# The FFN of a decoder block in two phases, each by Strassen's seven half products

## The chip, the cores and the metric

The kernel runs on one core of a Trainium2 chip. The metric is the device time of one execution in microseconds (us). Of the core's engines, TensorE (PE) multiplies matrices, VectorE (DVE), ScalarE (ACT) and GpSimd (POOL) work element by element, and SyncE (SP) issues the transfers (DMA). SBUF is the on-chip memory, PSUM holds TensorE's sums, DRAM is outside.

## The reference, cut to what matters

T = 1024 tokens, D = 1024. A layer norm and a mixer come first; the change leaves them as they are, up to the layer norm LN1. Then:

```
x = layer_norm(ALPHA * x + (1 + gt_a) * y, ln1_g, ln1_b)
h = x * (1 + sc_f) + sh_f
u = causal_dwconv(h @ w_up, conv_w) + conv_b      # [1024, 5632], three taps along the tokens
gate, val = split(u, 2, axis=-1)
y = (silu(gate) * val) @ w_down                   # [1024, 2816] @ [2816, 1024]
out = layer_norm(ALPHA * x + (1 + gt_f) * y, ln2_g, ln2_b)
```

## The kernel before

Every large product is done in three matmuls: each operand is split into a rounded part (hi) and a remainder (lo), and lo·hi, hi·lo and hi·hi are added in PSUM. Making a split costs a cast on ACT (L157) and a difference on POOL (L158).

LN1 ends in `ln1(t)` for the eight token tiles t; its last step is the ACT instruction L1198. `h2_of(t)` then transposes LN1's output on TensorE (L1207), scales it (L1214 on DVE, L1211 on ACT) into a tile of its own (`qm` or `km`), and splits it into `aH` and `aL`. The last two token tiles are transposed in the middle of the first matmuls of the FFN.

The FFN has 44 column blocks of w_up with 128 columns each: 22 gate blocks and 22 value blocks. `up_products` does one block: two token halves x 8 k-tiles x 3 matmuls of 128x512 (L1231 to L1233). `up` adds the convolution out of PSUM (ACT L1281, DVE L1284 twice), `pair(f)` does the silu (L1289), multiplies (L1291) and splits. `wdown` scales a block of w_down by the adaLN gate (L1300) and splits it. After every two f (four in the last group) the down products are done for all eight token tiles (L1334 to L1336) and added into `acc` (L1340; L1346 in the last group). `acc` already holds the residual, which POOL has made there (L1316, L1320). In the last group each tile's LN2 follows (L1346 to L1363). There are 2112 matmuls of 128x512 for the up products and 1056 (in their size) for the down products.

TensorE's order is that of the program; the other engines' instructions are placed by the framework's scheduler, and each engine runs its list in order. SP has one queue in order.

Of the kernel before, what the change touches and what calls it, by code (L numbers as in the profile page):

```python
# [88 lines left out]
def build(ctx, tc, out, cst, x, c, ln0_g, ln0_b, w_ada, b_ada, w_in, dn_conv, dn_a_log, dn_dt_bias,  # L89
# [1134 lines left out]
    ups = {}

    def up_products(blk, split=cols_of):
        hi, lo = split(w_up, blk * P)
        pp = ups[blk] = pup.tile([P, T], F32, tag="up", name=nm("up"), bufs=2)
        for sl in HS:
            for k in range(NK):  # L1230
                PE.matmul(pp[:, sl], lo[:, k, :], aH[:, k, sl], start=(k == 0), stop=False)  # L1231
                PE.matmul(pp[:, sl], hi[:, k, :], aL[:, k, sl], start=False, stop=False)  # L1232
# [152 lines left out]
```

## Time and profile before

| what | value |
|---|---|
| time, median of 3 runs | 1478.91 us (1477.97 to 1479.74) |
| span of the profiled execution | 1480.0 us |
| TensorE busy | 1414.6 us (96%) |
| DVE, ACT, POOL busy | 800.9, 452.0, 554.5 us |
| first matmul of the FFN, last matmul | 728.81, 1470.00 us |

The profiled execution is 1.1 us longer than the median. Busy time is what an engine spent in instructions, including what an instruction waited for inside itself. A share of the whole span averages over the mixer (up to 728 us), where several engines are busy, and the FFN.

### The profile page before, as it was taken

How to read it: one execution, taken by the hardware profiler on the slowest of the kernel's cores; microseconds unless marked ns; L12 is line 12 of the kernel's file. 1: busy time of each engine (PE TensorE's matmuls, PEld its weight loads, DVE VectorE, ACT ScalarE, POOL GpSimd, SP SyncE). 2: the span in 40 equal slices, each digit the busy share in tenths (PEclk: the TensorE clock that was granted, in tenths of full speed). 3: DMA queues.
4: the chain of work that ended last, by engine and by line, in shares of the span. 5: the costliest groups of instructions: out<-in, count | busy, mean ns of one | idle time of the engine just before them, and what ended most of it. 6: DMA issues, size and time to landing. Idle time of an engine off the chain costs nothing.

```text
span 1480.0 us, 17961 instructions
## 1 busy us (share of the span) xinstructions
PE 1414.6 (96%) x7037; PEld 1130.3 (76%) x7037; DVE 800.9 (54%) x1557; ACT 452.0 (31%) x658; POOL 554.5 (37%) x334
## 2 busy tenths in 40 slices
PE   6796999999998999999999999999999999999997
PEld 4565777788786787778778888888888888888886
DVE  7876954677447235867944343434434343434348
ACT  4356221233334432532541212121221212121322
POOL 2674211121115775431347374133231324133235
PEclk9888999999988998999999999999999999999999
DMA  9556312131204553353021212011111102011103
GB/s 320 148 155 187 70 39 57 32 81 33 69 11 157 179 176 114 122 165 99 15 69 39 64 43 71 29 58 57 44 50 36 58 29 71 29 58 56 30 15 114
DMA packets 144090, 120.20 MB, mean 81 GB/s; under 512 B 24067, under 2 KB 119167, under 8 KB 144005
## 3 DMA queue, kind: packets, MB, share of 16 engines
q1 hardware_dynamic: 144005, 119.05, 26.6%
q8 instruction: 55, 0.90, 0.3%
q14 instruction: 30, 0.25, 0.1%
HBM read 104.05 MB, written 14.98 MB: 80 GB/s over the span
## 4 chain that ended last, share of the span: by engine, by line
PE 78%; DVE 15%; issue 2%; ACT 1%; POOL 1%; DMA 1%; SPq 0%; POOLq 0%; DVEq 0%; ACTq 0%
PE up L1233 11%; PE up L1231 11%; PE up L1232 11%; PE pp L622 6%; PE pp L624 5%; PE pp L623 5%; PE down L1336 5%; PE down L1335 5%; PE down L1334 5%; DVE rq L139 1%; DVE mac L236 1%; DVE rq L140 1%; PE dn L864 1%; DVE ob L651 1%; PE pp L1182 1%
## 5 line engine op out<-in xcount | busy, mean ns | idle before, releaser
L158 POOL TENSOR_TENSOR wlo<-wst,whi 128x1024 fp32r<-128x1024 f32 x71 | 171.2, 2413 | 380.3 <-ACT whi L157 379.8
L1231 PE MATMUL up<-aH,wlo 128*128 128x512 f32 x688 | 272.2, 396 | 0.0
L1232 PE MATMUL up<-aL,whi 128*128 128x512 f32 x688 | 271.8, 395 | 0.0
L1233 PE MATMUL up<-aH,whi 128*128 128x512 f32 x688 | 271.8, 395 | 0.0
L622 PE MATMUL pp<-aH,wlo 128*128 128x512 f32 x432 | 191.2, 442 | 8.4 <-DVE ob L651 6.5
L1340 DVE TENSOR_TENSOR ob<-down,ob 128x512 f32<-128x512 f32 x144 | 97.0, 689 | 171.0 <-PE down L1336 168.9
L1284 DVE SCALAR_TENSOR_TENSOR cv<-up,colC,cv 128x1023 f32<-128x1023 f32 x88 | 112.8, 1281 | 126.0 <-ACT cv L1281 124.4
L624 PE MATMUL pp<-aH,whi 128*128 128x512 f32 x432 | 177.1, 410 | 0.0
L623 PE MATMUL pp<-aL,whi 128*128 128x512 f32 x432 | 176.4, 408 | 0.0
L1232 PEld LDWEIGHTS up<-aL,whi 128*128 128x128 f32 x688 | 129.8, 189 | 30.3
L1233 PEld LDWEIGHTS up<-aH,whi 128*128 128x128 f32 x688 | 129.8, 189 | 30.3
L1231 PEld LDWEIGHTS up<-aH,wlo 128*128 128x128 f32 x688 | 129.9, 189 | 30.2
L1281 ACT ACTIVATE cv<-up,colC 128x1024 f32<-128x1024 f32 x44 | 53.1, 1207 | 265.6 <-PE up L1233 265.6
L1336 PE MATMUL down<-wdhi,ghi 128*128 128x512 f32 (+1 forms) x322 | 125.9, 391 | 0.0
L1335 PE MATMUL down<-wdhi,glo 128*128 128x512 f32 (+1 forms) x322 | 125.7, 390 | 0.0
L1334 PE MATMUL down<-wdlo,ghi 128*128 128x512 f32 (+1 forms) x322 | 121.1, 390 | 0.0
L158 POOL TENSOR_TENSOR wdlo<-wdst,wdhi 128x1024 fp32r<-128x1024 f32 x20 | 56.8, 2841 | 143.9 <-ACT wdhi L157 143.9
L622 PEld LDWEIGHTS pp<-aH,wlo 128*128 128x128 f32 x432 | 85.3, 197 | 30.0 <-DVE ob L651 5.4
L624 PEld LDWEIGHTS pp<-aH,whi 128*128 128x128 f32 x432 | 85.2, 197 | 20.5
L623 PEld LDWEIGHTS pp<-aL,whi 128*128 128x128 f32 x432 | 85.7, 198 | 14.2 <-issue 0.5
L157 ACT CAST whi<-wst 128x1024 fp32r<-128x1024 f32 x71 | 73.9, 1041 | 53.7 <-issue 23.9
L1300 DVE TENSOR_TENSOR wdst<-wdst,gate 128x1024 f32<-128x1024 f32 x22 | 27.5, 1248 | 114.5 <-DMA wdst<-in_ffn_w_down 114.5
(451 smaller groups left out, 2338.2 us busy)
## 6 DMA issues: line engine op xcount, KB each, us to landing
wst<-in_ffn_w_up SPq DMA_DIRECT2D x44, 512.0 KB, 3.8
wst<-in_w_in SPq DMA_DIRECT2D x28, 512.0 KB, 3.9
K<-in_w_ada SPq DMA_DIRECT2D x48, 256.0 KB, 3.4
wdst<-in_ffn_w_down SPq DMA_DIRECT2D x22, 512.0 KB, 3.5
wada<-in_w_ada SPq DMA_DIRECT2D x8, 1024.0 KB, 7.0
xt<-in_x SPq DMA_DIRECT2D x8, 512.0 KB, 9.1
ob<-in_w_ada SPq DMA_DIRECT2D x16, 256.0 KB, 4.3
qd<-in_x SPq DMA_DIRECT2D x16, 256.0 KB, 3.0
```

Of the source, the lines that this page charges most:

```text
L158: eng.tensor_tensor(lo, st, hi.bitcast(F32), op=ALU.subtract)
L622: PE.matmul(pp, lo[:, k, :], aH[:, k, sl], start=(k == 0), stop=False)
L623: PE.matmul(pp, hi[:, k, :], aL[:, k, sl], start=False, stop=False)
L624: PE.matmul(pp, hi[:, k, :], aH[:, k, sl], start=False, stop=(k == NK - 1))
L1231: PE.matmul(pp[:, sl], lo[:, k, :], aH[:, k, sl], start=(k == 0), stop=False)
L1232: PE.matmul(pp[:, sl], hi[:, k, :], aL[:, k, sl], start=False, stop=False)
L1233: PE.matmul(pp[:, sl], hi[:, k, :], aH[:, k, sl], start=False, stop=(k == NK - 1))
L1284: V.scalar_tensor_tensor(t[:, sh:], pp[:, :T - sh], w(j), t[:, sh:], op0=ALU.mult, op1=ALU.add)
L1334: PE.matmul(pds[sl], gh[:, ct(t)], wl[:, sl], start=(i == 0), stop=False)
L1335: PE.matmul(pds[sl], gw[:, ct(t)], wh[:, sl], start=False, stop=False)
L1336: PE.matmul(pds[sl], gh[:, ct(t)], wh[:, sl], start=False, stop=(i == len(grp) - 1))
L1340: V.tensor_tensor(o[:, sl], pds[sl], o[:, sl], op=ALU.add)
```

## The change

It replaces the FFN. Strassen's scheme makes the product of two 2x2 block matrices from seven half-size products in place of eight, and takes sums of blocks on both sides for it.

Phase 1 goes through the 22 f. The 2x2 blocks are: of h, two token halves and two k halves; of w_up, the k halves and the pair of gate block f and value block f. `product(f, i)` is one of the seven products, 4 k-tiles x 3 matmuls, in the order 1, 6, 2, 5, 7, 3, 4; products 2, 3 and 4 go on in the PSUM bank of 1, 5 and 7 after `carry` has read that. `weights(f + 1)` makes the sums of weight blocks and their splits one f ahead (four differences on DVE, five splits and that of the gate block). The operand sums of h are made once, ahead of f = 0, in `acc` itself, where h2 now lies transposed; LN1's output goes to DRAM first (`ax2`). `carry` collects on DVE and ACT into rows of `acc` (seven rows taken in turn, four for each f), does the convolution, silu and product, and for every odd f `sums` stores the seven left operands of the second phase to DRAM (`dS`), four of them after sums on POOL.

Phase 2 has 77 steps: seven products i, in the order 1, 5, 6, 7, 4, 3, 2, by eleven j, each with 4 token tiles x 3 matmuls. `entry(i, j)` loads the left operand from `dS`, loads and combines w_down blocks, and splits both; it runs five steps ahead of the matmuls. `residual` loads LN1's output again and adds the scaled sum to it. The last product goes token tile by token tile, with LN2 behind each.

```diff
-        h2 = mt([P, NK, P], "km" if t % 2 else "qm")
+        nc.sync.dma_start(rowt(ax2, t), xh)
...
+                    V.tensor_scalar(xh[:, ct(k)], pt[:, j, :], AB2[:, 0, k:k + 1], AB2[:, 1, k:k + 1],
+                                    op0=ALU.mult, op1=ALU.add)
+            if t >= NT // 2 and q == 0:
+                continue
+            qs = slice(q * 4, q * 4 + 4)
+            h2 = xh[:, HS[q]].rearrange("p (k c) -> p k c", c=P)
+            S.copy(aH[:, qs, ct(t)], h2)
+            eng = V if t >= NT - 2 else G
+            eng.tensor_tensor(aL[:, qs, ct(t)], h2, aH[:, qs, ct(t)].bitcast(F32), op=ALU.subtract)
...
+    def product(f, i, n):
+        if i in (2, 3, 4) and (f >= 3 or i != 2):
+            pb, first_ = prod[f, {2: 1, 3: 5, 4: 7}[i]], False
+        else:
+            pb, first_ = bank(n), True
+        prod[f, i] = pb
+        hi, lo = opB[f, i]
+        for k in range(4):
+            ah, al = opA[i](k)
+            o = pb if len(ah.shape) == 2 else pb.rearrange("p (t c) -> p t c", c=P)
+            for w, a, flags in ((lo, ah, (first_ and k == 0, False)), (hi, al, (False, False)), (hi, ah, (False, k == 3))):
+                PE.matmul(o, w[:, k, :], a, start=flags[0], stop=flags[1], skip_group_check=not first_)
...
+    def split_s(i, s, eng):
+        if i not in s_hi:
+            s_hi[i] = ft([P, 4, 512], "sh", 2, F32R)
+        s_lo = ft([P, 4, 512], "sl", 4, F32R)
+        S.copy(s_hi[i], s)
+        eng.tensor_tensor(s_lo, s, s_hi[i].bitcast(F32), op=ALU.subtract)
+        opA[i] = (lambda k, hi=s_hi[i], lo=s_lo: (hi[:, :, ct(k)], lo[:, :, ct(k)]))
+    V.tensor_tensor(A22, A21, A22, op=ALU.add)
+    split_s(5, A22, G)
+    V.tensor_tensor(A21, A11, A21, op=ALU.subtract)
+    V.tensor_tensor(A11, A22, A11, op=ALU.subtract)
+    split_s(6, A11, V)
+    split_s(7, A21, G)
+    V.tensor_tensor(A12, A12, A11, op=ALU.subtract)
...
+    def weights(f):
+        B12, B22 = ft([P, 4, P], "vq", 3), ft([P, 4, P], "vq", 3)
+        nc.sync.dma_start(B22, wcols(NF + f, 1))
+        nc.sync.dma_start(B12, wcols(NF + f, 0))
+        st = raw.pop(f) if f in raw else gate_block(f)
+        yield
+        T3 = t3_tile()
+        V.tensor_tensor(T3, B22, B12, op=ALU.subtract)
+        V.tensor_tensor(B12, B12, st[:, KH[0], :], op=ALU.subtract)
+        split_q(f, 3, B22)
+        yield
+        V.tensor_tensor(B22, B22, B12, op=ALU.subtract)
+        split_q(f, 6, B22)
+        yield
+        split_q(f, 5, B12)
+        V.tensor_tensor(B22, st[:, KH[1], :], B22, op=ALU.subtract)
+        yield
+        split_q(f, 7, T3)
+        yield
+        split_q(f, 4, B22)
+    dS = {i: dram.tile([NF // 2, P, 512], F32, name=f"dS{i}") for i in range(1, 8)}
...
+    def conv(blk, cb):
+        t = row()
+        w = lambda j: colC[:, j * 44 + blk:j * 44 + blk + 1]
+        S.activation(t, cb, AF.Identity, bias=w(3), scale=w(2))
+        for j in (1, 0):
+            sh = 2 - j
+            V.scalar_tensor_tensor(t[:, sh:], cb[:, :T - sh], w(j), t[:, sh:], op0=ALU.mult, op1=ALU.add)
+        return t
...
+    def sums(j):
+        e, o = gs.pop(2 * j), gs.pop(2 * j + 1)
+        a11, a21, a12, a22 = e[:, HS[0]], e[:, HS[1]], o[:, HS[0]], o[:, HS[1]]
+        for i, a in ((1, a11), (2, a12), (4, a22)):
+            nc.sync.dma_start(dS[i][j], a)
+        G.tensor_tensor(a22, a21, a22, op=ALU.add)
+        G.tensor_tensor(a21, a11, a21, op=ALU.subtract)
+        G.tensor_tensor(a11, a22, a11, op=ALU.subtract)
+        G.tensor_tensor(a12, a12, a11, op=ALU.subtract)
+        for i, a in ((6, a11), (7, a21), (5, a22), (3, a12)):
+            nc.sync.dma_start(dS[i][j], a)
...
+    def carry(f, i):
+        pb = prod[f, i]
+        add = lambda o, b: V.tensor_tensor(o, pb, b, op=ALU.add)
+        if i == 1:
+            S.copy(u4_, pb)
+        elif i == 2:
+            blocks[f, 0] = row()
+            if f >= 3:
+                S.copy(blocks[f, 0][:, HS[0]], pb)
+            else:
+                add(blocks[f, 0][:, HS[0]], u4_)
+        elif i == 6:
+            add(u2_, u4_)
+        elif i == 5:
+            add(u4_, u2_)
+        elif i == 7:
+            blocks[f, 1] = row()
+            add(blocks[f, 1][:, HS[1]], u4_)
+        elif i == 3:
+            add(blocks[f, 1][:, HS[0]], u2_)
+            blocks[f, 1] = conv(NF + f, blocks[f, 1])
+        else:
+            add(blocks[f, 0][:, HS[1]], u2_)
+            t = conv(f, blocks.pop((f, 0)))
+            S.activation(t, t, AF.Silu)
+            g = gs[f] = blocks.pop((f, 1))
+            V.tensor_tensor(g, g, t, op=ALU.mult)
+            if f % 2:
+                sums(f // 2)
...
+        for f in range(NF):
+            ahead = weights(f + 1) if f + 1 < NF else iter(())
+            for i in (1, 6, 2, 5, 7, 3, 4):
+                if i in (1, 2) and f < 3:
+                    if i == 1:
+                        carry(f, 1)
+                        carry(f, 2)
+                else:
+                    step(f, i)
+                next(ahead, None)
...
+    ORDER = (1, 5, 6, 7, 4, 3, 2)
...
+    def entry(i, j):
+        hi, lo = slot(i, j)
+        s = dt_([P, 512], "st", 8)
+        nc.sync.dma_start(s, dS[i][j])
+        r0, r1 = R0[:, j, :], R1[:, j, :]
+        if i in (6, 4, 3, 2):
+            b = dt_([P, 512], "bt", 6)
+            load_b(b, j, *{6: (1, 1), 4: (1, 0), 3: (1, 1), 2: (1, 0)}[i])
+        if i == 1:
+            load_b(r0, j, 0, 0)
+            b = r0
+        elif i == 5:
+            load_b(r1, j, 0, 1)
+            V.tensor_tensor(r1, r1, r0, op=ALU.subtract)
+            b = r1
+        elif i == 6:
+            V.tensor_tensor(r1, b, r1, op=ALU.subtract)
+            b = r1
+        elif i == 7:
+            V.tensor_tensor(r0, r1, r0, op=ALU.subtract)
+            b = r0
+        elif i == 4:
+            V.tensor_tensor(b, b, r1, op=ALU.subtract)
+        if i in (4, 3, 2):
+            V.tensor_tensor(b, b, gate[:, HS[i == 3]], op=ALU.mult)
+        S.copy(hi[:, HS[0]], s)
+        S.copy(hi[:, HS[1]], b)
+        G.tensor_tensor(lo[:, HS[0]], s, hi[:, HS[0]].bitcast(F32), op=ALU.subtract)
+        V.tensor_tensor(lo[:, HS[1]], b, hi[:, HS[1]].bitcast(F32), op=ALU.subtract)
+        ents[i, j] = hi, lo
...
+    def residual(o, t, half_):
+        r = dt_([P, 512], "xr", 2)
+        nc.sync.dma_start(r, ax2[t * P:(t + 1) * P, HS[half_]])
+        G.tensor_tensor(r, r, g1r[:, HS[half_]], op=ALU.mult)
+        G.tensor_tensor(r, r, b1r[:, HS[half_]], op=ALU.add)
+        V.tensor_tensor(o, o, gate[:, HS[half_]], op=ALU.mult)
+        G.tensor_tensor(o, o, r, op=ALU.add)
...
+        for i, j in steps[:AHEAD]:
+            entry(i, j)
+        n = AHEAD
+        for ii, i in enumerate(ORDER[:-1]):
+            pbs = [bank(ii % 2) for _ in range(4)]
+            if i == 5:
+                for t in range(4):
+                    residual(c11(t), t, 0)
+            elif i == 4:
+                for t in range(4):
+                    residual(c21(t), t + 4, 0)
+                    residual(c22(t), t + 4, 1)
+            elif i == 3:
+                for t in range(4):
+                    residual(c12(t), t, 1)
+            for j in range(NJ):
+                if n < len(steps):
+                    entry(*steps[n])
+                    n += 1
+                for t in range(4):
+                    matmuls(pbs[t], i, j, t)
+            for t in range(4):
+                collect(i, t, pbs[t])
+        while n < len(steps):
+            entry(*steps[n])
+            n += 1
+        for t in range(4):
+            parts = (HS[0],) if t < 3 else (slice(0, 256), slice(256, 512))
+            for sl in parts:
+                pb = bank(0)[:, :sl.stop - sl.start]
+                for j in range(NJ):
+                    matmuls(pb, 2, j, t, sl)
+                V.tensor_tensor(acc[:, t, sl], pb, acc[:, t, sl], op=ALU.add)
+                stats(t, sl, 512 if t < 3 else 256)
+            ln2(t, 2 if t < 3 else 4, CUT_EARLY if t < 3 else CUT)
```

POOL in the FFN before: its list in the middle of the FFN holds the remainders of weights (`wlo`, `wdlo`) and of the activation (`glo`).

```order
L158 TENSOR_TENSOR wlo_8148<-wst_8145,whi_8147 128x1024
L158 TENSOR_TENSOR wdlo_8220<-wdst_8216,wdhi_8219 128x1024
L1295 TENSOR_TENSOR glo_8082<-cv_8076,ghi_8081 128x1024
L158 TENSOR_TENSOR wlo_8354<-wst_8351,whi_8353 128x1024
L158 TENSOR_TENSOR wlo_8414<-wst_8411,whi_8413 128x1024
L1295 TENSOR_TENSOR glo_8206<-cv_8200,ghi_8205 128x1024
```

POOL after, in an even f of phase 1: `vl` is the remainder of a weight sum for the f ahead, `wlo` that of its gate block, and L1377 to L1380 are the four sums for the two f before (`ob` is `acc`).

```order
L158 TENSOR_TENSOR wlo_8870<-wst_8867,whi_8869 128x1024
L1377 TENSOR_TENSOR ob<-ob 128x512
L1332 TENSOR_TENSOR vl_8789<-vq_8726,vh_8788 128x512
L1378 TENSOR_TENSOR ob<-ob 128x512
L1332 TENSOR_TENSOR vl_8808<-gate,vh_8807 128x512
L1379 TENSOR_TENSOR ob<-ob 128x512
L1332 TENSOR_TENSOR vl_8828<-vq_8727,vh_8827 128x512
L1380 TENSOR_TENSOR ob<-ob 128x512
```

The sum whose result is stored to dS7 (L1378) stands behind the gate block's remainder, L1377 and a weight remainder.

DVE before, at the last token tile's transposes: after the scaling comes the remainder of h2 and then the work of the first blocks.

```order
L1214 TENSOR_SCALAR km_6392<-dn_6393,AB_77 128x128 x4
L1218 CAST aH<-km_6392 128x4x128
L1222 TENSOR_TENSOR aL<-km_6392,aH 128x4x128 x2
L1300 TENSOR_TENSOR wdst_6641<-wdst_6641,gate 128x1024
L1284 SCALAR_TENSOR_TENSOR cv_6495<-up_6325,colC,cv_6495 128x1023
```

DVE after, at the same place: `ob` is again `acc`, `sh` and `sl` are the split of an operand sum, `vq` are weight blocks.

```order
L1224 TENSOR_SCALAR ob<-dn_6376,AB_77 128x128 x4
L1343 TENSOR_TENSOR gate<-vq_6522,vq_6521 128x512
L1344 TENSOR_TENSOR vq_6521<-vq_6521,wst_6322 128x512
L1232 TENSOR_TENSOR aL<-ob,aH 128x4x128
L1347 TENSOR_TENSOR vq_6522<-vq_6522,vq_6521 128x512
L1304 TENSOR_TENSOR ob<-ob 128x4x512
L1306 TENSOR_TENSOR ob<-ob 128x4x512
L1307 TENSOR_TENSOR ob<-ob 128x4x512
L1310 TENSOR_TENSOR ob<-ob 128x4x512
L1301 TENSOR_TENSOR sl_6413<-ob,sh_6412 128x2048
L1387 TENSOR_TENSOR ob<-up_6433,ob 128x512
```

The four sums over 2048 elements and a remainder of the same width now stand ahead of the first sum out of PSUM.

POOL before, at the end of the program, has two instructions of LN2 for each token tile.

```order
L1359 TENSOR_TENSOR ob<-ob,gr_10437 128x512
L1362 TENSOR_TENSOR ob<-ob,br_10438 128x512
```

POOL after, at the start of its last 65 element-wise instructions, in product 3 of phase 2: L1509 is the remainder of a left operand, L1517, L1518 and L1520 are the residual (`xr`).

```order
L1520 TENSOR_TENSOR ob<-ob,xr_10548 128x512
L1509 TENSOR_TENSOR aL<-st_10728,aH 128x512
L1517 TENSOR_TENSOR xr_10560<-xr_10560,gr_1435_9540 128x512
L1509 TENSOR_TENSOR aL<-st_10749,aH 128x512
L1517 TENSOR_TENSOR xr_10566<-xr_10566,gr_1435_9540 128x512
L1518 TENSOR_TENSOR xr_10560<-xr_10560,br_1436_9541 128x512
L1509 TENSOR_TENSOR aL<-st_10770,aH 128x512
L1518 TENSOR_TENSOR xr_10566<-xr_10566,br_1436_9541 128x512
L1520 TENSOR_TENSOR ob<-ob,xr_10560 128x512
```

What POOL did in the middle of the FFN (the residual) now stands between the remainders of the last steps.

## Rows read from the trace of the kernel before

**Rows 1.** The page: busy time, transfer rate by slice, and the chain's shares.

```profile
PE 1414.6 (96%) x7037; PEld 1130.3 (76%) x7037; DVE 800.9 (54%) x1557; ACT 452.0 (31%) x658; POOL 554.5 (37%) x334
...
GB/s 320 148 155 187 70 39 57 32 81 33 69 11 157 179 176 114 122 165 99 15 69 39 64 43 71 29 58 57 44 50 36 58 29 71 29 58 56 30 15 114
...
PE 78%; DVE 15%; issue 2%; ACT 1%; POOL 1%; DMA 1%; SPq 0%; POOLq 0%; DVEq 0%; ACTq 0%
```

**Rows 2.** Stretches: busy us (instructions) by engine, granted clock, DMA share, GB/s.

```profile
core 0: us, PE busy (x) PEld busy (x) DVE busy (x) ACT busy (x) POOL busy (x), PEclk, DMA share, GB/s
760.00:1440.00 680.00, 679.94 (x2938) 552.45 (x2937) 270.25 (x280) 155.37 (x147) 245.27 (x99) 1.00 0.16 47
```

**Rows 3.** Timeline, FFN, DVE and POOL: start, us, engine, instruction, [idle before <-releaser].

```profile
829.78 1.27 DVE L1291 TENSOR_TENSOR cv<-cv,cv 128x1024 f32<-128x1024 f32 x1
829.93 3.38 POOL L158 TENSOR_TENSOR wdlo<-wdst,wdhi 128x1024 fp32r<-128x1024 f32 x1
...
833.27 2.40 POOL L1295 TENSOR_TENSOR glo<-cv,ghi 128x1024 fp32r<-128x1024 f32 x1
...
849.85 2.40 POOL L158 TENSOR_TENSOR wlo<-wst,whi 128x1024 fp32r<-128x1024 f32 x1 [8.67 <-ACT whi L157]
851.51 1.83 DVE L1291 TENSOR_TENSOR cv<-cv,cv 128x1024 f32<-128x1024 f32 x1
```

**Rows 4.** Timeline, LN2 of the last group, DVE and POOL.

```profile
1447.95 0.69 DVE L1346 TENSOR_TENSOR ob<-down,ob 128x512 f32<-128x512 f32 x1
...
1457.28 1.87 DVE L1357 SCALAR_TENSOR_TENSOR ob<-ob,bmv,gr 128x512 f32<-128x512 f32 x1
...
1445.41 1.76 POOL L1362 TENSOR_TENSOR ob<-ob,br 128x512 f32<-128x512 f32 x1
1447.13 1.29 POOL L1359 TENSOR_TENSOR ob<-ob,gr 128x512 f32<-128x512 f32 x1
...
1457.30 1.29 POOL L1362 TENSOR_TENSOR ob<-ob,br 128x512 f32<-128x512 f32 x1
```

**Rows 5.** Groups from 728 us on: busy us, mean ns, idle before.

```profile
L1231 PE MATMUL up<-aH,wlo 128*128 128x512 f32 x688 | 272.2, 396 | 0.0
...
L1334 PE MATMUL down<-wdlo,ghi 128*128 128x512 f32 x318 | 120.0, 391 | 0.0
L158 POOL TENSOR_TENSOR wlo<-wst,whi 128x1024 fp32r<-128x1024 f32 x41 | 98.8, 2409 | 247.7 <-ACT whi L157 247.7
L1340 DVE TENSOR_TENSOR ob<-down,ob 128x512 f32<-128x512 f32 x144 | 97.0, 689 | 171.0 <-PE down L1336 168.9 <-POOL wlo L158 1.5 <-POOL ob L1316 0.6
...
L157 ACT CAST whi<-wst 128x1024 fp32r<-128x1024 f32 x41 | 42.5, 1036 | 0.0
...
L1300 DVE TENSOR_TENSOR wdst<-wdst,gate 128x1024 f32<-128x1024 f32 x22 | 27.5, 1248 | 114.5 <-DMA wdst<-in_ffn_w_down 114.5
```

**Rows 6.** The chain that ended last, at the last token tile: start, us, what.

```profile
742.22 1.25 ACT ob L1198
743.51 1.10 PE dn L1207 x8
```

**Rows 7.** DMA issues: out<-in, count, KB each, median us to landing.

```profile
K<-in_w_ada SPq DMA_DIRECT2D x48, 256.0 KB, 3.4
...
ax<-qd SPq DMA_DIRECT2D x16, 256.0 KB, 3.3
...
out<-ob SPq DMA_DIRECT2D x14, 256.0 KB, 2.0
...
dQK<-km SPq DMA_DIRECT2D x1, 512.0 KB, 4.3
```

**Rows 8.** Timeline: TensorE's transposes of tile 6 and the wait ahead of them.

```profile
734.28 1.81 PE L1207 MATMUL dn<-ident,ob 128*128 128x128 f32 x8 [2.45 <-DVE km L1214]
```

**Rows 9.** Stretches around waits of TensorE (columns as rows 2).

```profile
454.00:461.00 7.00, 7.00 (x29) 6.08 (x28) 5.49 (x19) 0.58 (x1) 1.87 (x2) 0.55 0.25 78
...
734.00:735.00 1.00, 0.72 (x5) 0.48 (x5) 0.94 (x3) 1.00 (x4) 0.00 (x0) 0.79 0.00 0
735.00:738.00 3.00, 3.00 (x10) 2.54 (x10) 2.78 (x6) 2.45 (x6) 2.49 (x2) 0.50 0.00 0
```

**Rows 10.** Timeline, the end: last matmul, last issue of a store.

```profile
1470.00 0.28 PE L1336 MATMUL down<-whi,ghi 128*128 128x256 f32 x1
...
1476.43 0.33 SPq L1363 DMA_DIRECT2D out<-ob  x1
```

More of the change, by code (lines that the diff above doesn't have):

```diff
@@ L42 @@
 LAG = 2
-LATE_H2 = (4,12)
 DVE_MODS = ((1, 1), (2, 1), (3, 0), (3, 1))
@@ L1224, in build @@
[L1224 to L1232, printed above, removed]
-                PE.matmul(pp[:, sl], hi[:, k, :], aH[:, k, sl], start=False, stop=(k == NK - 1))
-                yield
+            h2 = xh[:, HS[q]].rearrange("p (k c) -> p k c", c=P)
@@ L1241, in build @@
                 h2_of(t - LAG)
-        first_ups = [up_products(0), up_products(NF)]
-        seq = [0] * NK + [1] * NK + [0] * NK + [1] * NK
-        at = dict(zip(LATE_H2, range(NT - LAG, NT)))
-        for i, u in enumerate(seq):
-            if i in at:
-                h2_of(at[i])
-            next(first_ups[u])
+        raw = {0: gate_block(0), 1: gate_block(1)}
+        product(0, 1, 0)
+        h2_of(NT - 2)
+        product(1, 1, 0)
+        h2_of(NT - 1)
     mix.close()
     ps_long.close()
-    rowp = ctx.enter_context(tc.tile_pool(name="rowp", bufs=1, reuse_waits="tile"))
@@ new lines, in step, with drained @@
+    def step(f, i, n=None):
+        product(f, i, (f + 1) % 2 if n is None else n)
+        carry(f, i)
+    def drained(gen):
+        for _ in gen:
+            pass
+    with tc.manual_schedule(engines={PE.engine}):
+        product(0, 2, 0)
+        drained(weights(0))
+        product(1, 2, 0)
+        raw[2] = gate_block(2)
+        product(2, 1, 1)
+        product(2, 2, 1)
+        for f in range(NF):
[8 more added lines that the diff above has]
+                next(ahead, None)
+            drained(ahead)
@@ L1258, in rows_of @@
         return gr, br
[L1260 removed]
+    NJ = NF // 2
+    R1 = dt_([P, NJ, 512], "R1")
+    g1r, b1r = rows_of(1, ln1_g[0], ln1_b[0])
     S.mul(g1r, g1r, ALPHA)
     S.mul(b1r, b1r, ALPHA)
[L1265 to L1272 removed]
@@ new lines, in residual, with matmuls @@
+    def residual(o, t, half_):
[5 more added lines that the diff above has]
+        G.tensor_tensor(o, o, r, op=ALU.add)
+    def matmuls(pb, i, j, t, cols=slice(0, 512)):
+        hi, lo = ents[i, j]
+        l_hi, l_lo, r_hi, r_lo = hi[:, ct(t)], lo[:, ct(t)], hi[:, HS[1]][:, cols], lo[:, HS[1]][:, cols]
+        PE.matmul(pb, l_hi, r_lo, start=(j == 0), stop=False)
+        PE.matmul(pb, l_lo, r_hi, start=False, stop=False)
+        PE.matmul(pb, l_hi, r_hi, start=False, stop=(j == NJ - 1))
@@ new lines, in build, with stats, ln2 @@
+    c11 = lambda t: acc[:, t, HS[0]]
+    c12 = lambda t: acc[:, t, HS[1]]
+    c21 = lambda t: acc[:, t + 4, HS[0]]
+    c22 = lambda t: acc[:, t + 4, HS[1]]
+    epsc = sm([P, 1], "epsc", bufs=1)
+    V.memset(epsc, EPS)
+    def stats(t, sl, bw):
+        for b0 in range(sl.start, sl.stop, bw):
+            V.bn_stats(stat2[:, t, b0 // bw, :], acc[:, t, b0:b0 + bw])
+    def ln2(t, nb, cut):
+        o = acc[:, t, :]
+        mv = sm([P, 2], "bmv")
+        V.bn_aggr(mv, stat2[:, t, 0:nb, :].rearrange("p a b -> p (a b)"))
+        rs = sm([P, 1], "brs")
+        S.activation(rs, mv[:, 1:2], AF.Sqrt, bias=epsc)
+        V.reciprocal(rs, rs)
+        nmr = sm([P, 1], "nmr")
+        V.scalar_tensor_tensor(nmr, mv[:, 0:1], -1.0, rs, op0=ALU.mult, op1=ALU.mult)
+        ca, cb = slice(0, cut), slice(cut, D)
+        V.scalar_tensor_tensor(o[:, ca], o[:, ca], mv[:, 0:1], g2r[:, ca], op0=ALU.subtract, op1=ALU.mult)
+        S.activation(o[:, cb], o[:, cb], AF.Identity, bias=nmr, scale=rs)
+        G.tensor_tensor(o[:, cb], o[:, cb], g2r[:, cb], op=ALU.mult)
+        V.scalar_tensor_tensor(o[:, ca], o[:, ca], rs, b2r[:, ca], op0=ALU.mult, op1=ALU.add)
+        nc.sync.dma_start(out[t * P:(t + 1) * P, ca], o[:, ca])
+        G.tensor_tensor(o[:, cb], o[:, cb], b2r[:, cb], op=ALU.add)
+        nc.sync.dma_start(out[t * P:(t + 1) * P, cb], o[:, cb])
```

195 lines of the change are left out of this document (91 added, 104 removed).

## The prediction

> **What bounds the kernel now.** I read the page first: TensorE is busy 96% of the span, the chain that ended last runs 78% through it, and VectorE (DVE) is busy 54%, GpSimd (POOL) 37% [rows 1]. The table by stretches then gives the FFN: from 760 to 1440 us TensorE never rests, at the upper clock level (2.4 GHz, granted 1.00), with 2938 matmuls on record in 680 us, so 0.2314 us for one [rows 2]. In the FFN the matmul count alone sets the time; DVE has 270 and POOL 245 us of work in these 680.
>
> The change issues 1848 + 924 = 2772 matmuls of 128x512 for 2112 + 1056 = 3168. The 396 fewer are worth 396 x 0.2314 = **91.7 us**, if all that is added stays under TensorE. What is added is work on DVE and POOL, so I looked next at how these two stand beside each other.
>
> **The rows that decide: DVE and POOL take turns.** Look at when each starts and ends [rows 3]. The product L1291 (two operands from SBUF) starts at 829.78 and ends at 831.05; the POOL instruction that starts at 829.93 takes 3.38 us, where its neighbour takes 2.40, and ends 2.26 after DVE's end. At 851.51 it is the other way: L1291 takes 1.83 and ends 1.09 after POOL's end at 852.25. In LN2 [rows 4], L1357 begins at 1457.28, takes 1.87, and ends 0.56 after POOL's end at 1458.59. But L1346, whose operands are PSUM and SBUF, takes 0.69 at 1447.95 in the middle of a POOL instruction, like the 0.689 mean of 144 such sums [rows 5]. So a DVE instruction with two SBUF operands and a POOL instruction don't run together, and a sum out of PSUM is free. From these rows a turn costs DVE 0.55 (512 wide) or 1.09 (1024), and POOL 1.17 behind a wait or 1.29 alone (512), 2.40 (1024). The kernel before has few of the first kind in the FFN; the change is made of them.
>
> The Trainium skill's page "SBUF — State Buffer" (section "SBUF: two separate sides") has this as an exclusive lock on a port pair, held for the whole instruction while the other fully blocks, and it speaks against this change. These rows agree on the order, but the loser loses less than the winner's whole time plus its own. With whole durations (POOL 1.29, DVE 0.69) phase 2 below would need 139 x 1.29 + 194 x 0.69 = 313 us of turns; by the rows' turns it needs 139 x 1.17 + 194 x 0.55 = 269. I take the rows.
>
> **The front.** Before, tile 7 is normalised by 743.47 and its transposes start at 743.51 [rows 6]; TensorE then has work without end. After, the operand sums need all of h2, and h2 overwrites LN1's output only when that has landed in DRAM. In ACT's list four casts of weight sums (L1331, 512 wide, 0.6 each: a little over half of L157's 1.04 [rows 5]) stand ahead of the normalisation (+2.5: 746); the 512 KB store lands after 4.3 (the one store of that size) [rows 7]: 751; overwriting 1.5: 752.5. Then DVE's list (the DVE rows of the change): three 2048-wide sums (2.45 each, twice L1300's 1.23 [rows 5]) with a 2048-wide POOL remainder (2 x 2.40) taking its turn between them, a cast (2 x 1.04), a fourth sum and the DVE remainder (2.4): 752.5 + 7.4 + 4.8 + 2.1 + 2.4 = 769, so product (0,6) starts at **770** (762 if POOL keeps out of the way, 774 if a second POOL remainder gets in). Only 72 matmuls are done by then.
>
> **Phase 1.** One f is 84 matmuls, 19.4 us. Its turns: DVE four 512-wide differences (2.3), four convolution steps, which now read SBUF, not PSUM (4 x 1.15), one product (1.1); POOL one 2.40 and five 1.29; 8.0 + 8.9 = 16.9, and 5.2 more for the four sums of every second f: 19.5 on average. That just fits, so a wait decides, in every even f. The sum of product 7 (L1387) goes into a row whose store to dS7 must have landed. The chain, from the start of f: the product of f-1 (L1411) ends at 9.6 (add, convolution, silu ahead of it); dS4 is issued at 10.1 and lands after 2.0 to 3.3 [rows 7]; POOL, behind the 2.40 of the gate block, does L1377 to 14.7, a weight remainder to 16.0, gives DVE a turn to 16.6, L1378 to 17.9 (the first POOL rows of the change); dS7 lands at about 20.6; the sum ends at 21.4. Product 4, due at 16.7, waits for it: **4.8 us** (3.3 without the turns, none if the store lands at once). Behind such a wait the clock falls: after the 2.45 us before 734.28 [rows 8] the granted clock was 0.79 and then 0.50 (1.2 GHz) up to 738 [rows 9]; a spell of 3.3 us costs 1.6. The odd f has slack and recovers. A pair: 38.9 + 4.8 + 1.6 = 45.3.
>
> f = 0, 1, 2 have five products each (13.9), but 17.5 us of turns, and f = 2 the dS7 wait, about 8.5 longer since product 4 is due earlier: 61. f = 3: 19.4. Nine pairs: 408. In 48 of 84 matmuls the moving operand lies in four pieces of 128 columns, which no row before shows; its bounds are 0 and, by the spread of the groups' means (391 to 396 ns) [rows 5], 1056 x 0.005 = 5 us; I take 0, since the pace follows the columns. Phase 1 ends at 770 + 1.6 + 61 + 19.4 + 408 = **1260**. The first entry of phase 2 waits for the last matmul (the buffers' memory is shared), then a load of 256 KB (3.4 [rows 7]), a cast (0.6) and a remainder (0.7): 5.0, and 1.6 of clock: **1266.6**.
>
> **Phase 2.** 77 steps of 12 matmuls, 2.78 us each, 214. A step's operands need one POOL turn and one (i = 1), two, or three (i = 4) DVE turns: 1.72, 2.27, 2.82; a residual (16 of them) 3 POOL and 1 DVE: 4.06; LN2 of a tile 3.44. Steps 0 to 54 with what POOL's list has among them (four residuals, four POOL turns of two more, eight sums of quarters, the last sums of phase 1): 18.9 + 74.9 + 31.0 + 16.2 + 4.7 + 4.4 + 4.7 = 155, TensorE 153: it keeps up until about 157. Behind it stand 65 POOL instructions (their list begins in the second POOL rows of the change): 22 steps (50), the rest of the residuals (44), eight tiles of LN2 (27.5): 121.5 us of turns for 61 us of matmuls. So TensorE waits for remainders, and phase 2 takes 157 + 121.5 + 1.5 = **280 us** (228 if nothing but TensorE and POOL's own list bound it: 214, a 6 us wait at the last product, 8 of LN2 behind the last residual; 313 by whole durations). In the tail before, the last matmul is at 1470.00 and the last store's issue at 1476.43 [rows 10]; that piece stays inside the 280. The loads, some 37 MB in 280 us or 132 GB/s, hide: the page's first slice moves 320 [rows 1].
>
> **Sum.** 1266.6 + 280 = 1546.6 on the profiled span of 1480.0, which is 1.1 over the median 1478.91: **1545 us**, 4.5% slower. Against 1480.0 - 91.7 = 1388 that is 158 more: the front 20 (some 156 matmuls were issued by 770, now 72) and 1.6 of clock, f = 0 to 2 19, even f 9 x 6.4 = 58, transition 7, phase 2 280 - 214 - 10 of tail that was there before = 56; the sum, 161, is off by rounding.
>
> **Rivals.** (1) TensorE stays the bound and turns cost nothing where it matters: front 767, f = 0 to 2 52, pairs 38.9 + 3.3 + 1.6 = 43.8, phase 2 228: 767 + 1.6 + 52 + 19.4 + 394 + 6.6 + 228 = 1469, **faster**; with the dS7 wait hidden too, 1420. For it: POOL's 37%. Against it: [rows 3, 4]. It decides once phase 2 has less than about 210 us of turns. (2) The scheduler's mixing of the lists lets half of phase 2's surplus pass (DVE's sums out of PSUM and TensorE's five steps of lead cover turns): 280 becomes 254, pairs 43.8: **1505**. (3) Whole durations, as the Trainium skill's page just named has it: 313 in phase 2, **1578**; [rows 3, 4] show less. (4) Clock spells of 7 us behind each wait, as seen from 454 to 461 [rows 9]: 1.9 more, fourteen times: 1572.
>
> **How the numbers follow.** The forecast (1515 to 1570) gets 0.47, rival 2 (1480 to 1515) 0.24, rival 1 0.17, (3) and (4) together 0.09, and 0.03 falls within 0.2% of the time before, about what a measurement of this kernel can tell from no change. The range takes the forecast, rivals 2 to 4 and the top of rival 1: 1468 to 1585. Faster 0.17, same 0.03, slower 0.80.
>
> **What would show it.** TensorE idle before L1264 in every second f, 4 to 5 us, released by L1387, itself by a dS7 store; clock 0.50 behind; pairs of f 45 us apart. In phase 2 DVE L1506 and L1510 far over 0.69 on average, DVE's and POOL's two kinds of spans side by side, and TensorE idle in the last 120 us, released by L1509 or L1510. I am wrong if L1510 is at 0.69 with POOL busy, or if TensorE is above 95% after 1270.

## The result, and the profile after

The changed kernel takes 1564.3 us (median of 4, 1563.1 to 1569.1) against 1479.3 us: a ratio of 1.060, interval 1.057 to 1.063. It is 5.7 to 6.3% slower. The forecast was 1545 (1468 to 1585). The profiled execution takes 1565.4 us, its span is 1563.3.

The page, to be held against [rows 1]: TensorE's share falls from 96 to 87%, DVE's rises from 54 to 69%, POOL's from 37 to 52%, and the chain that ended last now runs 23% through DVE and 9% through POOL.

```profile
PE 1366.8 (87%) x6662; PEld 1076.9 (69%) x6662; DVE 1078.4 (69%) x1778; ACT 576.2 (37%) x910; POOL 805.8 (52%) x530
...
PE 53%; DVE 23%; POOL 9%; DMA 6%; issue 5%; ACT 2%; SPq 0%; DVEq 0%; POOLq 0%; ACTq 0%
```

TensorE is now busy 47.8 us less, not 91.7: part of its matmuls run at the lower clock, where one starts every 0.43 us and not every 0.23. Its waits from 728 us on say for whom it stands (total, times, longest):

```profile
PE up L1264 <- DVE ob L1387: 55.3, 12, 11.0
PE up L1526 <- POOL aL L1509: 27.2, 11, 14.8
PE up L1525 <- DVE aL L1510: 20.8, 10, 9.3
...
PE up L1264 <- ACT sh L1300: 7.3, 1, 7.3
PE up L1264 <- DVE sl L1301: 6.0, 1, 6.0
```

The table by stretches (columns as [rows 2]), where 760 to 1440 before had no gap at granted 1.00: front, f = 0 to 2, the rest of phase 1, the transition, phase 2.

```profile
728.00:770.00 42.00, 25.02 (x99) 19.11 (x97) 33.23 (x55) 19.88 (x30) 22.66 (x11) 0.79 0.25 78
770.00:838.00 68.00, 46.78 (x178) 36.63 (x178) 49.68 (x43) 21.23 (x26) 34.70 (x21) 0.83 0.24 74
838.00:1268.30 430.30, 390.15 (x1600) 311.62 (x1598) 247.44 (x260) 160.54 (x202) 218.59 (x143) 0.95 0.27 84
1268.30:1277.60 9.30, 0.00 (x0) 0.03 (x1) 7.90 (x8) 7.27 (x11) 2.50 (x2) 0.65 1.01 381
1277.60:1563.30 285.70, 230.23 (x957) 182.18 (x957) 261.76 (x256) 98.65 (x178) 251.34 (x144) 0.89 0.47 157
```

Three places show the mechanism. **The front**, timeline of DVE, POOL and TensorE: DVE's sums over 2048 elements take 2.29 alone and 6.5 beside a POOL remainder of the same width. The first of these remainders takes 4.70, the second, which waits for a sum, 6.56. Two get in, not one.

```profile
758.62 2.29 DVE L1306 TENSOR_TENSOR ob<-ob 128x2048 f32<-128x2048 f32 x1
760.60 4.70 POOL L1301 TENSOR_TENSOR sl<-ob,aH 128x2048 fp32r<-128x2048 f32 x1 [6.77 <-ACT aH L1300]
760.94 6.51 DVE L1307 TENSOR_TENSOR ob<-ob 128x2048 f32<-128x2048 f32 x1
765.26 6.56 POOL L1301 TENSOR_TENSOR sl<-ob,aL 128x2048 fp32r<-128x2048 f32 x1
767.48 6.50 DVE L1310 TENSOR_TENSOR ob<-ob 128x2048 f32<-128x2048 f32 x1
776.24 0.80 PE L1264 MATMUL up<-sl,vh 128*128 128x512 f32 x1 [6.01 <-DVE sl L1301]
```

**An even f of phase 1**, the same view with SP's queue. TensorE waits 4.78 us here, and the same in seven other even f (waits that end at 879.72 to 1202.97).

```profile
918.50 1.29 POOL L1332 TENSOR_TENSOR vl<-vq,vh 128x512 fp32r<-128x512 f32 x1
...
919.82 0.38 SPq L1339 DMA_DIRECT2D vq<-in_ffn_w_up  x1
...
921.07 2.77 SPq L1382 DMA_DIRECT2D dS<-ob  x2
...
922.23 1.26 POOL L1379 TENSOR_TENSOR ob<-ob 128x512 f32<-128x512 f32 x1
922.81 1.23 DVE L1343 TENSOR_TENSOR gate<-vq,vq 128x512 f32<-128x512 f32 x1 [6.04 <-DMA vq<-in_ffn_w_up]
923.45 1.71 POOL L1332 TENSOR_TENSOR vl<-vq,vh 128x512 fp32r<-128x512 f32 x1
924.13 1.58 DVE L1344 TENSOR_TENSOR vq<-vq,wst 128x512 f32<-128x512 f32 x1
...
925.63 0.68 DVE L1387 TENSOR_TENSOR ob<-up,ob 128x512 f32<-128x512 f32 x1
926.37 0.79 PE L1264 MATMUL up<-aH,vl 128*128 128x512 f32 x1 [4.78 <-DVE ob L1387]
```

Read it from below. L1387 starts when L1344 ends; L1344 follows L1343; both give POOL a turn (1.58 and 1.23 for 0.69). L1343 had waited 6 us for a weight load that was issued at 919.82, when POOL's remainder L1332 freed the buffer. The dS7 store was issued at 921.07. By the rows of f = 2 below, where the sum starts 2.1 us after that issue, it landed at about 923.2, while DVE was at L1343. The wait has the forecast size, but its last link is another.

In f = 2, where TensorE's wait is the longest (10.98, to 834.02), and in the last even f (1.92, to 1245.68), the last link is the forecast one: the sum starts when the store has landed.

```profile
831.16 0.32 SPq L1382 DMA_DIRECT2D dS<-ob  x1
...
833.27 0.69 DVE L1387 TENSOR_TENSOR ob<-up,ob 128x512 f32<-128x512 f32 x1 [4.61 <-DMA dS<-ob]
```

**Phase 2**, groups (busy, mean ns | idle before). The sums out of PSUM (L1559) are at 680 ns; the remainder L1509 is at 1659, the two-operand differences at 1291 to 1538, where a DVE instruction of 128x512 alone takes 0.69 us.

```profile
L1509 POOL TENSOR_TENSOR aL<-st,aH 128x512 fp32r<-128x512 f32 x74 | 121.7, 1659 | 43.2 <-ACT aH L1507 40.8 <-DMA bt<-in_ffn_w_down 1.3 <-DMA st<-dS 1.0
L1510 DVE TENSOR_TENSOR aL<-R,aH 128x512 fp32r<-128x512 f32 x44 | 66.0, 1538 | 1.0 <-ACT aH L1508 1.0
...
L1506 DVE TENSOR_TENSOR bt<-bt,gate 128x512 f32<-128x512 f32 x33 | 45.9, 1410 | 0.8 <-DMA bt<-in_ffn_w_down 0.6
...
L1559 DVE TENSOR_TENSOR ob<-up,ob 128x512 f32<-128x512 f32 x16 | 10.6, 680 | 2.9 <-POOL ob L1520 2.9
```

### The profile page after: what moved, and what is told of

Read it like the earlier page. It is cut to its first block, busy times and chain, and to the rows that moved or that the text cites. A ratio compares the mean times of both kernels' runs of the same rounds, so it can differ in the third digit from the quotient of the medians.

```text
span 1563.3 us, 18816 instructions
## 1 busy us (share of the span) xinstructions
PE 1366.8 (87%) x6662; PEld 1076.9 (69%) x6662; DVE 1078.4 (69%) x1778; ACT 576.2 (37%) x910; POOL 805.8 (52%) x530
## 4 chain that ended last, share of the span: by engine, by line
PE 53%; DVE 23%; POOL 9%; DMA 6%; issue 5%; ACT 2%; SPq 0%; DVEq 0%; POOLq 0%; ACTq 0%
PE up L1264 22%; PE pp L622 5%; PE pp L623 5%; PE pp L624 5%; DVE aL L1510 2%; POOL ob L1520 2%; POOL vl L1332 1%; DMA bt<-in_ffn_w_down 1%; DVE bt L1506 1%; DMA dS<-ob 1%; POOL wlo L158 1%; DVE rq L139 1%; PE dn L864 1%; DVE mac L236 1%; DVE rq L140 1%
## 5 line engine op out<-in xcount | busy, mean ns | idle before, releaser
L1332 POOL TENSOR_TENSOR vl<-vq,vh 128x512 fp32r<-128x512 f32 x88 | 132.7, 1510 | 169.9 <-ACT vh L1331 164.9
L624 PE MATMUL pp<-aH,whi 128*128 128x512 f32 x432 | 176.6, 409 | 0.0
L1526 PE MATMUL up<-aH,aL 128*128 128x512 f32 (+1 forms) x304 | 122.7, 404 | 27.3 <-POOL aL L1509 27.2
L1525 PE MATMUL up<-aL,aH 128*128 128x512 f32 (+1 forms) x304 | 122.6, 403 | 25.8 <-DVE aL L1510 20.8
L1264 PE MATMUL up<-sl,vh 128*128 128x512 f32 x352 | 139.8, 397 | 6.0 <-DVE sl L1301 6.0
L1509 POOL TENSOR_TENSOR aL<-st,aH 128x512 fp32r<-128x512 f32 x74 | 121.7, 1659 | 43.2 <-ACT aH L1507 40.8
L1387 DVE TENSOR_TENSOR ob<-up,ob 128x512 f32<-128x512 f32 x113 | 77.2, 686 | 95.0 <-PE up L1264 75.7
L1366 DVE SCALAR_TENSOR_TENSOR ob<-ob,colC 128x1023 f32<-128x1023 f32 (+1 forms) x88 | 121.5, 1384 | 13.3 <-ACT ob L1363 12.4
L1264 PE MATMUL up<-aH,vl 128*128 128x512 f32 x176 | 78.4, 445 | 51.1 <-DVE ob L1387 51.1
L1527 PE MATMUL up<-aH 128*128 128x512 f32 (+1 forms) x304 | 120.5, 396 | 0.0
L624 PEld LDWEIGHTS pp<-aH,whi 128*128 128x128 f32 x432 | 85.1, 197 | 20.8
L1525 PEld LDWEIGHTS up<-aL,aH 128*128 128x128 f32 x304 | 59.6, 196 | 44.2 <-DVE aL L1510 22.7
L1264 PEld LDWEIGHTS up<-sl,vh 128*128 128x128 f32 x352 | 66.9, 190 | 22.0 <-DVE sl L1301 6.5
L1264 PEld LDWEIGHTS up<-aH,vl 128*128 128x128 f32 x176 | 37.1, 211 | 63.8 <-DVE ob L1387 55.3
```

The lines of the kernel that those rows point to most:

```text
L624: PE.matmul(pp, hi[:, k, :], aH[:, k, sl], start=False, stop=(k == NK - 1))
L1264: PE.matmul(o, w[:, k, :], a, start=flags[0], stop=flags[1], skip_group_check=not first_)
L1332: G.tensor_tensor(lo, q, hi.bitcast(F32), op=ALU.subtract)
L1366: V.scalar_tensor_tensor(t[:, sh:], cb[:, :T - sh], w(j), t[:, sh:], op0=ALU.mult, op1=ALU.add)
L1387: add = lambda o, b: V.tensor_tensor(o, pb, b, op=ALU.add)
L1509: G.tensor_tensor(lo[:, HS[0]], s, hi[:, HS[0]].bitcast(F32), op=ALU.subtract)
```

## The experiments

**e1, e5, e7: DVE and POOL by themselves.** Small programs of 128x512 instructions, in place of the whole computation: POOL adds `a` and `b`, DVE adds `c` and `d` (two SBUF operands) or `q` (PSUM) and `d`. e1 and e5 set eight POOL instructions beside a stream on DVE (the code in short, the loops of e5 written out):

```
for _ in range(8):  G.tensor_tensor(pa, a, b, op=ALU.add)
for k in range(24): V.tensor_tensor(va, c, d, op=ALU.add)        # e1: one tile
for k in range(24): V.tensor_tensor(four[k % 4], c, d, op=ALU.add)  # e5: four tiles
for _ in range(16): V.tensor_tensor(va, q, d, op=ALU.add)        # e1: out of PSUM
```

> A kernel that leaves the whole computation out and only runs instructions of 128x512 in stretches of their own: 8 POOL sums alone; 12 DVE sums of two SBUF operands alone; then 8 POOL sums each time beside 24 DVE sums of two SBUF operands without a pause, 16 DVE sums of PSUM and SBUF, 12 DVE sums that each wait for an ACT copy, 16 DVE products of one SBUF operand with a constant, and 10 pairs of an SBUF and a PSUM sum. If DVE and POOL take turns (the prediction's reading): alone 1.29 and 0.62 us each; beside 24 DVE sums the two need 8 x 1.17 + 24 x 0.57 = 23 us together, and since DVE kept POOL standing for 14.8 us in phase 2 of the changed kernel, POOL stands until DVE pauses; beside the PSUM sums each keeps its own pace (8 x 1.29 = 10.3, 16 x 0.69 = 11); with ACT copies between, DVE's sums wait about 1 us each for POOL. If the long spans have another cause (the queue, a DMA, the clock): 15 us for the stretch of 24, POOL at 1.29 and DVE at 0.62 throughout.

The timeline of e1; POOL's eight alone took 10.64 us, twelve DVE sums alone 0.724 apart:

```profile
25.41 13.08 POOL L32 TENSOR_TENSOR pa<-a,b 128x512 f32<-128x512 f32 x8
26.68 23.98 DVE L56 TENSOR_TENSOR va<-c,d 128x512 f32<-128x512 f32 x24
51.02 10.67 POOL L32 TENSOR_TENSOR pa<-a,b 128x512 f32<-128x512 f32 x8
...
86.63 1.37 DVE L72 TENSOR_SCALAR va<-c 128x512 f32<-128x512 f32 x1
96.42 0.43 DVE L72 TENSOR_SCALAR va<-c 128x512 f32<-128x512 f32 x1
```

Beside two-operand sums POOL goes from 10.64 to 13.08; beside the sums out of PSUM it stays at 10.67, and these at 0.690 each (16 of them). So turns exist for two SBUF operands, and not for a sum out of PSUM. A product of one SBUF operand with a constant (L72) takes turns as well: seven of its 16 last 1.37, the nine others 0.41 to 0.43, and their mean of 0.837 hides it; POOL's eight take 11.14 beside them. Sums that each waited for an ACT copy lasted 0.99 beside POOL, 0.3 more and not 1 us more as expected. I had expected POOL to stand still until DVE pauses, and that was wrong: the two alternate.

> DVE and POOL alone again, 512 wide, the whole computation is left out. The question is when POOL stands still behind DVE, as it did for 14.8 us in phase 2, where DVE's two-operand sums wrote different tiles and began 0.60 us apart at 0.68 each, while beside sums that all wrote one tile (0.72 apart) POOL got every second turn. Theory A: it is the missing gap; sums into four tiles in turn then shut POOL out: beside 24 of them (14.5 us) POOL's eight last about 14 + 10 = 24 us and DVE keeps its 14.5; the single POOL instruction behind a first sum takes 10 us or more, while 20 sums run; sums into one tile alternate again (DVE 24, POOL 13 us). Theory B: it is something else of phase 2 (a transfer, the tiles' places): then both streams alternate, some 24 us for DVE's 24 sums whatever they write, POOL's eight in 13, and the single POOL instruction takes under 2.5.

```profile
16.20 14.54 DVE L49 TENSOR_TENSOR v<-c,d 128x512 f32<-128x512 f32 x24
...
31.11 13.00 POOL L34 TENSOR_TENSOR pa<-a,b 128x512 f32<-128x512 f32 x8
...
32.30 21.98 DVE L49 TENSOR_TENSOR v<-c,d 128x512 f32<-128x512 f32 x24
```

Theory A of e5 falls: a gapless DVE stream (14.54 for 24 alone, 0.60 apart) also lets POOL in at every second place, and the single POOL instruction took 1.58. The price of a turn can be read here: from 31.11 to 54.28 both streams take 23.17 us, so each of the eight POOL instructions adds (23.17 - 14.54) / 8 = 1.08 to DVE's 0.61, and a pair takes 1.08 + 0.61 = 1.69. The prediction's rows gave 1.17 + 0.55 = 1.72, whole durations 1.29 + 0.69 = 1.98. The Trainium skill's page "SBUF — State Buffer" (section "SBUF: two separate sides") has the loser blocked for the winner's whole instruction. The order agrees, and so does the exemption of the sums out of PSUM; the price by the runs is 0.29 lower than two whole durations.

> DVE and POOL alone, the whole computation is left out. Each part: DVE makes a tile, one POOL instruction (512 wide) waits for it, and 20 DVE instructions follow at once without a wait. Parts: a as in the run before (tiles of its own), b DVE in place, c POOL in place, d both in place, e both in place with DVE's rounded differences in between (as in phase 2), f as d with two more POOL instructions. If working in place is what shut POOL out in phase 2: a 1.6 us for the POOL instruction, and 12 to 14 in those parts where it matters (b, d, e, or c, d, e), with the DVE instructions at 0.60 apart without a break. If it isn't: 1.3 to 2 us for every POOL instruction in all six parts, and the cause of that one stall stays open.

All eight POOL instructions of e7's six parts took 1.58 to 1.71 us: working in place isn't what held POOL up in phase 2 either (see the last section).

**e2: rows apart.** Stored products get rows of their own for four f; temporaries get fixed rows.

```diff
-    def conv(blk, cb):
-        t = row()
+    def conv(blk, cb, n):
+        t = row(n)
...
-            blocks[f, 0] = row()
+            blocks[f, 0] = row(4)
...
-            blocks[f, 1] = row()
+            blocks[f, 1] = row(5)
...
-            blocks[f, 1] = conv(NF + f, blocks[f, 1])
+            blocks[f, 1] = conv(NF + f, blocks[f, 1], f % 4)
...
-            t = conv(f, blocks.pop((f, 0)))
+            t = conv(f, blocks.pop((f, 0)), 6)
```

> The changed kernel, with the rows of the collected blocks apart: three fixed rows for what lives within one f, and the four others only for the products that wait to be stored (f mod 4), so that the sum of product 7 never waits for a store to dS7. If the wait for that store makes the stall in every even f (prediction): no wait before L1264 released by L1387 of 4.8 us, the clock at 1.00 through phase 1, a pair of f falls from 46.2 to 40 to 42 us, and f = 2 loses its 11 us: 9 x 5 + 11 + 1.6 off 1564, about 1505 (1495 to 1520). If turns between DVE and POOL fill phase 1 anyway (19.5 us of turns per f) and the wait only shows them: the wait moves to another instruction, 1545 or more. If the store's landing is not what is waited for: 1564.

1525.2 us, ratio 1.033 (1.029 to 1.037): 39 us less than the changed kernel, where 59 were expected, so it lies between the two cases. The 4.78 us waits are gone, but of the 15.2 us of waits on L1387 ahead of f = 3 (10.98 of them in f = 2) 11.2 stay. Timeline of the same place in another even f:

```profile
995.80 0.69 DVE L1387 TENSOR_TENSOR ob<-up,ob 128x512 f32<-128x512 f32 x1 [2.07 <-PE up L1264]
...
998.05 1.48 DVE L1343 TENSOR_TENSOR gate<-vq,vq 128x512 f32<-128x512 f32 x1 [1.56 <-DMA vq<-in_ffn_w_up]
...
1005.93 0.50 PE L1264 MATMUL up<-aH,wlo 128*128 128x512 f32 x1 [1.80 <-ACT ob L1389]
```

Free of the store, the sum stands ahead of L1343 in DVE's list. L1343 still waits for its load, and L1343, L1344 and the convolution still give turns (1.48, 1.61, 2.31 in this f); the delay comes out later, as 11 waits of 0.5 to 2.9 on L1389, 17.0 us together.

**e3: phase 2 without POOL**, its 141 instructions on DVE (139 of them 512 wide): the same edit in `entry`, `residual` and `ln2`.

```diff
-        G.tensor_tensor(lo[:, HS[0]], s, hi[:, HS[0]].bitcast(F32), op=ALU.subtract)
+        V.tensor_tensor(lo[:, HS[0]], s, hi[:, HS[0]].bitcast(F32), op=ALU.subtract)
...
-        G.tensor_tensor(o, o, r, op=ALU.add)
+        V.tensor_tensor(o, o, r, op=ALU.add)
...
```

> The changed kernel, with all 139 POOL instructions of phase 2 given to DVE, nothing else. If DVE and POOL take turns: POOL's 139 x 1.17 = 163 us of turns become 139 x 0.62 = 86 on DVE, which then has 333 x 0.62 + 36 x 0.69 = 231 us of work without waits; phase 2 falls from 286 to about 240 (230 to 250), the time to about 1518 (1505 to 1530), and DVE's sums are at 0.68 on average. If DVE is simply short of time in phase 2 (busy 259 of 280 us there) and POOL's work lies beside it: 86 us more on the busier engine, phase 2 of about 345, 1620.

1522.5 us, ratio 1.030 (1.027 to 1.033): as expected. Phase 2 takes 243.0 us for 285.7, L1510 is at 688 to 731 ns and no wait on L1509 is left, while phase 1 keeps its waits on L1387 (55.0 us). DVE has 396 instructions in phase 2 for 256, yet its busy time falls from 261.8 to 230.5: DVE's long spans were turns, not a load of its own.

**e6: phase 1 without POOL**, the seven rows in turn kept.

```diff
-        hi, lo = split_w(st, [P, NK, P])
+        hi, lo = split_w(st, [P, NK, P], eng=V)
...
-    split_s(5, A22, G)
+    split_s(5, A22, V)
...
-    split_s(7, A21, G)
+    split_s(7, A21, V)
...
-        G.tensor_tensor(lo, q, hi.bitcast(F32), op=ALU.subtract)
+        V.tensor_tensor(lo, q, hi.bitcast(F32), op=ALU.subtract)
...
-        G.tensor_tensor(a22, a21, a22, op=ALU.add)
+        V.tensor_tensor(a22, a21, a22, op=ALU.add)
...
```

> Phase 1's POOL work (weight remainders, four sums for every second f, two of the front) on DVE; the seven rows in turn and phase 2 stay as they are. The prediction put the even-f wait at 4.8 us with turns and 3.3 without, and the rest of phase 1 at TensorE's pace. If the turns make the chain to dS7 late: waits on L1387 in even f fall from 4.8 to between 1.0 and 3.3 us, first phase-2 matmul between 1222 and 1240 (1277.6 before, 1205.2 where the rows are apart as well), median 1507 to 1527. If the reuse of rows alone sets the wait: it stays at 4 to 5 us, first phase-2 matmul 1250 or later, median 1535 to 1555. If the turns alone do: no wait is left, 1206 to 1215, median 1490 to 1502.

1511.5 us, ratio 1.023 (1.021 to 1.025), phase 2 from 1224.9: the first case. Of 4.78 in an even f 1.1 to 2.0 stay. The sum still stands behind L1343 and L1380 in DVE's list (rows below); in two of the eight, DVE then also stands 0.35 and 0.91 us for the store. The wait of f = 2 stays whole, 11.70 for 10.98, with the store as its last link.

```profile
947.59 0.69 DVE L1343 TENSOR_TENSOR gate<-vq,vq 128x512 f32<-128x512 f32 x1 [0.59 <-DMA vq<-in_ffn_w_up]
948.20 0.69 DVE L1380 TENSOR_TENSOR ob<-ob 128x512 f32<-128x512 f32 x1
...
949.96 0.50 PE L1264 MATMUL up<-aH,vl 128*128 128x512 f32 x1 [1.59 <-DVE ob L1387]
```

**e4: all three together**; of its work in the FFN, POOL keeps two remainders of h2 ahead of f = 0.

> Both of the edits before, and phase 1's POOL work (weight remainders, the gate block's remainder, the four sums, two operand remainders) on DVE as well, so that POOL is idle in the FFN. If turns are the cause: DVE has 3.4 + 5.0 + 2.5 + 1.2 + 3.1 + 1.2 + 1.2 = 17.7 us of work in an f of 19.4, pairs of 39 to 41, phase 2 of 240, the front some 5 us shorter: 1445 (1430 to 1470), under the time before the change. If DVE is the engine that is short: phase 1 and 2 both grow, 1600 or more.

1448.5 us, ratio 0.980 (0.977 to 0.983): 1.7 to 2.3% faster than the kernel before. From 838 to 1196 TensorE doesn't rest, at granted 1.00 (stretches), though DVE is busy 86% of it:

```profile
838.00:1196.30 358.30, 358.30 (x1542) 289.24 (x1540) 308.91 (x392) 153.98 (x194) 0.00 (x0) 1.00 0.31 100
1205.20:1448.00 242.80, 217.25 (x957) 178.25 (x957) 228.63 (x400) 101.56 (x178) 0.00 (x0) 0.94 0.57 186
```

The length of phase 1 in the four runs separates its two causes. It is counted from the first matmul of the FFN (L1264) to the first of phase 2 (L1525), since the four profiled executions reach the FFN at 729.0, 724.4 (e2), 731.0 (e6) and 731.7 (e4). That spread begins in the mixer, which the edits leave alone (its last L624 starts at 623.7, 620.6, 623.4 and 624.6):

| phase 1, us | POOL works | its work on DVE |
| --- | --- | --- |
| seven rows in turn | 548.6 | 493.9 |
| rows apart | 513.3 | 473.5 |

POOL's work costs 54.7 with the reuse and 39.8 without it; the reuse 35.3 with POOL's work and 20.4 without: together 75.1. With phase 2's 42.9 (285.7 to 242.8), less the 2.7 by which e4 reaches the FFN later, that is 115.3 us, all of 1563.3 - 1448.0. Moving the work to DVE does two things: the turns go, and a POOL instruction of 1.29 becomes a DVE instruction of 0.69. For phase 1 these runs don't part the two.

## Why the prediction was right

The forecast case came: TensorE lost what 396 fewer matmuls gave, to DVE and POOL taking turns and to waits in every even f. Its parts, against the span: 1546.6 forecast, 1563.3 measured, 16.7 more, of which phase 1 8.3, the transition 2.7, phase 2 5.7. Neither of its signs of being wrong came: L1510 is at 1291 to 1538 ns with POOL busy, and TensorE is busy 81% of phase 2.

- **The front.** The first matmul of product (0,6) was forecast at 770 and came at 769.4, but the next waited until 776.2: DVE's own remainder L1301 (`sl`) stood behind L1310, which a second POOL remainder held to 6.50. The prediction named that as its 774 and took 770, and its sum has no term for L1310, the fourth sum that it names.
- **The even f.** The wait of 4.8 us was measured as 4.78, in the place that the prediction named and in eight of the nine even f from f = 4 on. The agreement is luck: the chain "dS7 lands at about 20.6; the sum ends at 21.4" is not what ended last there. POOL was faster than forecast: with product 4 due at 921.6, 16.7 us into this f, the store was issued 16.2 into it, not 17.9. The reuse does two things: the sum depends on the store, and the scheduler puts it behind L1343 and L1344, which stand ahead of it in DVE's list and which the prediction did not follow. These wait for a weight load that POOL's remainder gates. With the store landed at about 923.2, the store alone would have cost some 2.5 us by these rows (an estimate); the other 2.3 are L1343 and L1344. "3.3 without the turns" was too high as well: e6 has 1.1 to 2.0.
- **The clock.** "a spell of 3.3 us costs 1.6" was right behind every second of these waits and too small behind the others. After the waits that end at 879.72, 971.99, 1064.16 and 1156.37 the granted clock stayed at 0.50 (1.2 GHz) for some 5.7 us, after the four between them for some 3.4 (stretches):

```profile
879.72:885.43 5.71, 5.71 (x13) 4.46 (x14) 2.16 (x3) 1.38 (x2) 0.47 (x1) 0.50 0.27 90
885.43:887.00 1.57, 1.57 (x8) 1.30 (x7) 1.57 (x2) 1.45 (x2) 1.01 (x1) 1.00 0.00 0
926.37:929.80 3.43, 3.43 (x8) 2.75 (x9) 1.62 (x2) 1.24 (x1) 0.46 (x1) 0.50 0.46 150
929.80:931.50 1.70, 1.70 (x8) 1.37 (x8) 0.84 (x2) 0.44 (x1) 0.00 (x0) 1.00 0.00 0
```

  Thirteen matmuls in 5.71 us are 2.7 us more than at 0.2314 each, eight in 3.43 are 1.6 more: 38.9 + 4.8 + 2.7 = 46.4 and 38.9 + 4.8 + 1.6 = 45.3, where the pairs measured 46.6 and 45.6 in turn (46.2 on average).
- **The transition.** 9.3 us for 5.0 (whose three terms add up to 4.7) and a clock spell: DVE was busy 7.9 of it, with the last convolution and its product (L1366, L1411) ahead of the remainder that TensorE waited for. In e4 it is still 8.9.
- **Phase 2.** 280 forecast, 285.7 measured, and 242.8 to 243.0 without POOL (15 more than the prediction's 228 without turns: e4's TensorE still waits for L1510, and there is the tail). The prediction "keeps up until about 157", then loses some 60, was wrong in its shape: of 43.7 us of waits behind the first matmul one of 14.8, which no term had, ended at 1338, 61 us into phase 2; from 1440 on TensorE was idle 36.8 of 123, the tail included. So the 280 came near as a total, not as an account of where the time goes. TensorE's busy time rose to 230.2 from e4's 217.3, with the clock at 0.89 on average for 0.94.
- **The rivals.** That turns cost nothing where it matters (1469) falls with e3 and e6. Half the surplus passing (1505) lies far below. By the number alone, whole durations (1578) and seven-us clock spells (1572) come nearer to 1564.3 than 1545 does; what speaks against them is e5's 1.69 for a pair, on the side of the rows that were taken, and the spells of 5.7 and 3.4 in turn, 4.6 on average.

## What to carry to other kernels

Fewer matmuls pay only if what they are exchanged for doesn't make two engines wait for each other: count the DVE sums and products that read SBUF alone and stand beside POOL work, 1.7 us for a pair of 128x512 with two operands, before counting matmuls. When such pairs are the limit, try everything on the faster of the two: here, with the rows apart, DVE alone did the work of both and TensorE stopped waiting in phase 1 from 838 us on. And follow a wait through the list of its engine: a reused buffer also moves the instruction behind others, whose own waits then count.
